# Gate and up products of two SwiGLU half steps by seven block products for eight, with the hidden tiles through DRAM to a down phase of its own

## The chip, the cores and the metric

The kernel runs on one core of a Trainium2 chip. The metric is the device time of one execution in microseconds (us). Its engines are named as in the profile: PE (TensorE, matmuls), DVE (VectorE), ACT (ScalarE), POOL (GpSimd) and SP (SyncE, which here only issues DMAs). The matmuls write into eight PSUM banks of 128 partitions by 512 float32; everything else lies in SBUF or DRAM.

## The reference

One residual block over 1024 tokens of 1024 channels, all in float32:

```python
x = x + 0.5 * swiglu(rmsnorm(x, ffn1_norm), ffn1_w_gate, ffn1_w_up, ffn1_w_down)
x = x + hybrid_mixer(rmsnorm(x, mix_norm), w_in, conv_w, conv_b, sb_out_norm, conv_out_norm, w_out)
x = x + 0.5 * swiglu(rmsnorm(x, ffn2_norm), ffn2_w_gate, ffn2_w_up, ffn2_w_down)
return rmsnorm(x, final_norm)

def swiglu(h, w_gate, w_up, w_down):
    return (silu(h @ w_gate) * (h @ w_up)) @ w_down
```

`w_gate` and `w_up` are 1024 by 2816, `w_down` is 2816 by 1024. The mixer projects to q, k, v and three convolution streams (`w_in`, 1024 by 3072), does stick-breaking attention in 8 heads of 64 and a short causal convolution over 512 channels, norms both groups, and projects back with `w_out` (1024 by 1024).

## The kernel before

**Arithmetic.** A float32 operand is split into a high part, rounded to the format float32r that PE multiplies (a CAST on ACT, line 173), and the remainder (a subtraction on DVE, line 174). A product of two operands is three matmuls, high by high, high by low, low by high (`mm3` and `both`, lines 220 to 244); each is 128 by 128 by 512 and they add up in one PSUM bank. All matmuls of the main stream are issued in `mm`, line 95.

**FFN.** Channels lie on the partitions, tokens along the row, in two halves of 512 (`hf`). The 2816 hidden channels are 22 tiles of 128, in five chunks (`CHUNKS`). For a tile `m`, `ffn` makes the gate product and then the up product, over 8 tiles of input channels and both halves (`both`): 2 x 8 x 2 x 3 = 96 matmuls into four banks. `gated` reads gate from PSUM (lines 422 to 424), `hidden` multiplies by up (432) and splits the result into an `h` tile. At the end of a chunk its down product is made for each of 8 tiles of output channels and added to the residual (463). In the second FFN the last chunk's down product has rows of tokens (`down_by_rows`), with the residual transposed on PE (`to_rows`, 891) one chunk earlier, and each row goes through the final norm and out; the very last piece is 256 columns wide.

**Norm.** `Norm.feed` splits the residual times the gain (180) without waiting for the rms. 1/rms follows through a chain of small steps (`Rms`: sums, columns, diagonals, broadcast, rows) and arrives as a row in every partition (the copy of line 312); `gated` multiplies by it. For the mixer, `rescale` scales the tiles themselves later (327).

**Weights.** `Stream` holds the order of all weight tiles. A tile of 128 by 1024 is loaded on SP's DMA queue into one of three `raw` slots and split into one of two pairs `whi`, `wlo`, one tile ahead.

**Order.** The kernel's text lays side chains between the matmuls at distances (`after`). The order on each engine's queue is made by a planner from the text's order and from when it reckons that operands and slots are ready: an instruction that isn't ready may be passed by a later one. `behind` fixes an order where it must hold. A slot of a pool is given again once all readers of its last tile are done.

**Memory.** 32 `act` slots of 512 columns (2 KB a partition) hold the split activations, 18 `h` slots of 1024 columns the hidden tiles, the residual, v, q and k, 18 `t` slots of 512 what is temporary.

## Time and profile before

| | us |
|---|---|
| median of 3 runs | 1979.15 |
| lowest, highest run | 1977.16, 1981.97 |
| span of the profiled execution | 1980.5 |
| PE busy | 1965.7 |
| weight loads (PEld) busy | 1633.7 |
| DVE busy | 931.5 |
| ACT busy | 666.3 |
| POOL busy | 46.4 |

The page gives the profiled execution no time beside its span; the span lies between the lowest and the highest run. A row of a group names the line, engine, operation, output and inputs with their shapes, how many there are, their busy time together, the mean of one in ns, and the idle time of the engine ahead of them with what ended it. A row of a window gives the stretch in us, its length, then for each engine its busy time in the stretch with the number of its instructions, the granted clock of PE, the share of the DMA engines and GB/s. A row of the timeline gives start, duration, engine, line, operation and tiles; a DMA's row among the issues gives the number, the size and the median us from issue to landing. Matmuls are pipelined, so the duration shown for one is longer than the distance between two, and the distance is what counts.

### The profile page before, as it was taken

To read this page: it belongs to the slowest core of one execution; us is meant where nothing else is said; L and a number is where in the kernel's file an instruction comes from. 1 tells how busy PE (TensorE), PEld (TensorE's weight loads), DVE (VectorE), ACT (ScalarE), POOL (GpSimd) and SP (SyncE) were. 2 spreads that over 40 slices of the span, in tenths; PEclk is the share of its full clock that TensorE was granted. 3 is DMA by queue.
4 is the path that set the end of the run, shared out by engine and by line. 5 is a ranking of instruction groups with operands and counts; after the bars stand their busy time and mean duration, and the time that the engine had idled before them with its cause. 6 is when DMAs were issued, how large, how long until landed. Compare 5 with 4: busy or idle time off the path is not lost.

```text
span 1980.5 us, 22183 instructions
## 1 busy us (share of the span) xinstructions
PE 1965.7 (99%) x8932; PEld 1633.7 (82%) x8932; DVE 931.5 (47%) x1541; ACT 666.3 (34%) x1212; POOL 46.4 (2%) x78
## 2 busy tenths in 40 slices
PE   9999999999999999999999999999999999999998
PEld 7888888888888888788888888888888888888887
DVE  6423233333333277568787898433333233333335
ACT  6311121111211155467677775321111121112223
POOL 0000000000000000100101000000000000000001
PEclk9999999999999999999999999999999999999999
DMA  5112112102112042332405222211211211201212
GB/s 160 40 39 67 47 34 63 48 27 75 32 47 65 28 160 85 83 78 56 96 27 128 91 93 65 64 35 40 64 50 33 67 43 33 74 27 52 61 43 86
DMA packets 181287, 124.15 MB, mean 63 GB/s; under 512 B 5392, under 2 KB 167488, under 8 KB 181184
## 3 DMA queue, kind: packets, MB, share of 16 engines
q1 hardware_dynamic: 177344, 113.29, 19.2%
q0 software_dynamic: 3840, 9.44, 2.4%
q8 instruction: 70, 1.15, 0.2%
q14 instruction: 33, 0.27, 0.0%
HBM read 102.00 MB, written 11.27 MB: 57 GB/s over the span
## 4 chain that ended last, share of the span: by engine, by line
PE 99%; issue 1%; DMA 0%; ACT 0%; DVE 0%; SPq 0%; POOL 0%; POOLq 0%
PE ps L95 97%; PE ps L276 0%; PE ps L891 0%; PE ps L479 0%; DMA raw<-in_ffn_w_up 0%; PE ps L304 0%; PE ps L306 0%; PE ps L307 0%; POOL sm L930 0%; ACT t L935 0%; POOLq L961 0%; DVE wlo L499 0%; DVE act L180 0%; ACT whi L496 0%; ACT t L312 0%
## 5 line engine op out<-in xcount | busy, mean ns | idle before, releaser
L95 PE MATMUL ps<-act,whi 128*128 128x512 f32 x3648 | 1037.3, 391 | 2.4 <-ACT act L179 1.6
L95 PEld LDWEIGHTS ps<-act,whi 128*128 128x128 f32 x3648 | 682.1, 188 | 139.4 <-ACT act L179 1.8
L95 PE MATMUL ps<-act,wlo 128*128 128x512 f32 x1824 | 600.0, 390 | 0.0
L173 ACT CAST whi<-raw 128x1024 fp32r<-128x1024 f32 (+2 forms) x200 | 183.1, 915 | 1107.2 <-PE ps L95 1066.0
L95 PEld LDWEIGHTS ps<-act,wlo 128*128 128x128 f32 x1824 | 342.9, 188 | 68.1 <-DVE wlo L174 0.4
L95 PE MATMUL ps<-h,whi 128*128 128x512 f32 x1344 | 362.6, 389 | 0.0
L95 PEld LDWEIGHTS ps<-h,whi 128*128 128x128 f32 x1344 | 252.1, 188 | 52.7 <-ACT h L173 0.3
L174 DVE TENSOR_TENSOR wlo<-raw,whi 128x1024 fp32r<-128x1024 f32 (+2 forms) x200 | 209.5, 1047 | 25.3 <-ACT whi L173 25.2
L463 DVE SCALAR_TENSOR_TENSOR h<-ps,h 128x512 f32<-128x512 f32 x144 | 92.8, 686 | 265.5 <-PE ps L95 265.4
L95 PE MATMUL ps<-h,wlo 128*128 128x512 f32 x672 | 209.5, 389 | 0.0
L422 DVE TENSOR_TENSOR t<-t,ps 128x512 f32<-128x512 f32 x88 | 56.5, 684 | 316.3 <-PE ps L95 316.3
L432 DVE TENSOR_TENSOR t<-t,ps 128x512 f32<-128x512 f32 x80 | 51.5, 684 | 281.4 <-PE ps L95 281.3
L95 PEld LDWEIGHTS ps<-h,wlo 128*128 128x128 f32 x672 | 126.1, 188 | 26.2
L762 ACT ACTIVATE t<-ps 128x128 f32<-128x128 f32 (+2 forms) x96 | 47.0, 489 | 43.9 <-PE ps L95 43.4
L95 PE MATMUL ps<-h,h 128*128 128x128 f32 (+2 forms) x192 | 57.8, 357 | 3.3 <-issue 3.3
L774 DVE TENSOR_TENSOR t<-t,ps 128x128 f32<-128x128 f32 (+2 forms) x96 | 52.8, 550 | 16.7 <-ACT t L770 16.3
L424 DVE TENSOR_TENSOR t<-t,t 128x512 f32<-128x512 f32 x88 | 56.7, 685 | 4.0 <-ACT t L423 4.0
L174 DVE TENSOR_TENSOR h<-t,h 128x512 fp32r<-128x512 f32 x89 | 57.4, 685 | 1.0 <-ACT h L173 1.0
L770 ACT ACTIVATE t<-t 128x128 f32<-128x128 f32 (+2 forms) x96 | 50.2, 523 | 19.1 <-DVE t L766 17.8
L807 DVE TENSOR_TENSOR t<-ps,t 128x128 fp32r<-128x128 f32 (+2 forms) x96 | 52.9, 551 | 4.7 <-ACT ps L803 4.1
L788 DVE TENSOR_TENSOR t<-t,t 128x128 fp32r<-128x128 f32 (+2 forms) x96 | 53.1, 553 | 3.7 <-ACT t L784 3.3
L173 ACT CAST h<-t 128x512 fp32r<-128x512 f32 x89 | 52.4, 618 | 4.8 <-DVE t L432 4.8
(126 smaller groups left out, 1334.2 us busy)
## 6 DMA issues: line engine op xcount, KB each, us to landing
raw<-in_ffn_w_gate SPq DMA_DIRECT2D x43, 512.0 KB, 3.9
raw<-in_ffn_w_up SPq DMA_DIRECT2D x43, 512.0 KB, 3.9
raw<-in_w_in SPq DMA_DIRECT2D x28, 512.0 KB, 4.0
raw<-in_ffn_w_down SPq DMA_DIRECT2D x32, 320.0 KB, 3.2
raw<-in_ffn_w_down SPq DMA_DIRECT2D x40, 256.0 KB, 2.8
h<-h POOLq DMA_DIRECT2D x24, 256.0 KB, 5.0
raw<-in_w_out SPq DMA_DIRECT2D x12, 512.0 KB, 3.4
h<-in_x SPq DMA_DIRECT2D x8, 512.0 KB, 7.3
```

The source lines that it names most:

```text
L95: nc.tensor.matmul(out, lhs, rhs, **kw)
L173: nc.scalar.copy(hi, x)
L174: nc.vector.tensor_tensor(out=lo, in0=x, in1=f(hi), op=ALU.subtract)
L422: nc.vector.tensor_tensor(out=s[hf], in0=rms, in1=g[hf], op=ALU.mult)
L424: nc.vector.tensor_tensor(out=s[hf], in0=s[hf], in1=rms, op=ALU.mult)
L432: nc.vector.tensor_tensor(out=s[hf], in0=s[hf], in1=u[hf], op=ALU.mult)
L463: nc.vector.scalar_tensor_tensor(out=x, in0=o[hf], scalar=0.5, in1=x, op0=ALU.mult, op1=ALU.add)
L762: behind(nc.scalar.activation(u["s"][:, cols], u["z"][:, cols], AF.Exp), table_set)
L770: nc.scalar.activation(sc, sc, AF.Ln, bias=1.0)
L774: nc.vector.tensor_tensor(out=sc, in0=sc, in1=u["z"][:, cols], op=ALU.max)
L788: nc.vector.tensor_tensor(out=u["sl"][:, cols], in0=u["s"][:, cols], in1=f(u["sh"])[:, cols], op=ALU.subtract)
L807: nc.vector.tensor_tensor(out=u["al"][:, cols], in0=u["z"][:, cols], in1=f(u["ah"])[:, cols], op=ALU.subtract)
```

## The change

**Gate and up.** In each FFN the first two hidden tiles are made as before (`STD`); in the first FFN the very first of them still runs under the transposes of the input. For the other 20 tiles, gate and up of one tile, two halves of the input channels and two halves of the tokens are seen as a 2 by 2 by 2 block product. It is made by seven products of blocks (`P1`, `P2`, `P3`, `P5`, `P6`, `P7`, `Q4`) of 4 channel tiles each, 7 x 4 x 3 = 84 matmuls, in place of eight. The right operands are sums and differences of the activations, scaled by gain and 1/rms in place, and split: 7 x 4 pairs, made once in each FFN by `right`. The left operands are sums of the four blocks of a tile's gate and up weights, made for each tile by `left` in steps, one step behind each product of the tile before. The seven products go into four banks: P2 adds to P1's, Q4 to P7's, P3 to P5's, each after the part that is there has been read (`Unit.do`). The first two Strassen tiles of a phase run product by product together (`ALL`), while the right operands are made; the others one by one (`FEW`).

**Hidden tiles.** They are stored unsplit to DRAM (`h_sp`) on POOL's DMA queue. When all 22 are made, `down` reads them back in pairs, splits them (`down_prep`) and makes all of the down product in fourteen steps (`TURNS`), each with two output tiles and up to four pairs of hidden tiles. In the first FFN the outputs are channels by tokens; in the second they are rows of tokens throughout, on the residual that `to_rows` has transposed and stored to DRAM (`r_sp`) at the end of the mixer.

**Residual.** The input's tiles are stored to DRAM at the start (`x_sp[0]`) and read back at the first four down steps (`x_back`), since `right` overwrites them.

**Slots.** The pools `act`, `h` and `t` become one pool `s` of 72 slots of 512 columns; the weights' parts are 10 slots `w` of 1024 columns; `raw` is 2 slots of 2048 columns, and a weight load can be 1 MB. q, k and their parts are tiles of one token half, and their copies between partitions are twice as many of half the size. Two of the eight v tiles lie in `s`.

```diff
-    def big(tag, bufs, dt=F32, shape=(P, S)):
-        return sb.tile(list(shape), dt, name=nm(tag), tag=tag, bufs=bufs)
-    def act_tile(dt=F32R):
-        return big("act", 32, dt, (P, HALF))
-    def h_tile(dt=F32R):
-        return big("h", 18, dt)
-    def tmp(dt=F32):
-        return big("t", 18, dt, (P, HALF))
+    def s(dt=F32):
+        return sb.tile([P, HALF], dt, name=nm("s"), tag="s", bufs=72)
+    def w4(dt=F32R):
+        return sb.tile([P, S], dt, name=nm("w"), tag="w", bufs=10)
...
+            raw = sb.tile([P, 2 * S], F32, name=nm("raw"), tag="raw", bufs=2)
+            for c0, n, view, src in spec:
+                nc.sync.dma_start(out=view(raw[:, c0 : c0 + n]), in_=src)
...
+    h_sp = [dr.tile([NF, P, S], F32, name=f"h_sp{i}") for i in range(2)]
+    NQ = NF // 2
+    TURNS = [(i % 4, max(0, i - 3), min(NQ, i + 1)) for i in range(NQ + 3)]
...
+            yield [part(j * S, w[:, m * P : (m + 1) * P]) for j, w in enumerate((wg, wu))]
+        h = h_sp[i].rearrange("f p c -> (f p) c")
+        ring, rows = (wd, h) if i else (h, wd)
+        for j, (g, q0, q1) in enumerate(TURNS):
+            if j < NQ:
+                yield [part(0, ring[2 * j * P : 2 * (j + 1) * P])]
+            yield [part(k * (q1 - q0) * 2 * P, rows[2 * q0 * P : 2 * q1 * P, (g + 4 * k) * P : (g + 4 * k + 1) * P])
+                   for k in range(2)]
...
-    def ffn(act, started, scale, last, done):
...
-        for c in range(5):
-            h = []
-            for m in range(CHUNKS[c], CHUNKS[c + 1]):
...
-                run(both(g, W(), NK, act))
...
-                s = gated(g, act)
-                run(both(u, W(), NK, act))
-                h.append(hidden(s, u, scale if c == 4 else None))
...
-            for d in range(NK):
-                w = W()
                 o = [bank(), bank()]
-                run(both(o, w, len(h), lambda k, hf: tuple(a[:, hs(hf)] for a in h[k])))
...
+    def left(raw):
+        a = {}
+        def blk(i, n=1):
+            return raw[:, i * HALF : (i + n) * HALF]
+        def halves(hi, lo, *names):
+            for i, n in enumerate(names):
+                a[n] = (hi[:, i * HALF : (i + 1) * HALF], lo[:, i * HALF : (i + 1) * HALF])
+        def two(ap):
+            return ap.rearrange("p (n c) -> p n c", c=HALF)
+        yield a
+        halves(*split(w4(), w4(), blk(0, 2)), "P2", "P1")
+        yield
+        y = w4(F32)
+        nc.vector.tensor_tensor(out=two(y), in0=two(blk(1, 2)), in1=blk(3).unsqueeze(1).to_broadcast([P, 2, HALF]),
+                                op=ALU.add)
+        nc.vector.tensor_tensor(out=blk(3), in0=y[:, :HALF], in1=blk(2), op=ALU.add)
+        nc.vector.tensor_tensor(out=blk(0), in0=blk(3), in1=blk(0), op=ALU.add)
+        yield
+        z = two(raw)[:, 0::3]
+        hi, lo = w4(), w4()
+        split(two(hi), two(lo), z)
+        halves(hi, lo, "P3", "P6")
+        yield
+        halves(*split(w4(), w4(), y), "P7", "P5")
+        yield
+        a["Q4"] = split(s(F32R), s(F32R), blk(2))
+        L.load()
+        yield
+    def right(x, y):
+        b = {}
+        yield b
+        def parts(name, tiles):
+            b[name] = [split(s(F32R), s(F32R), a) for a in tiles]
+        def comb(out, i, j, op):
+            nc.vector.tensor_tensor(out=out, in0=i, in1=j, op=op)
+            return out
+        def four(k0, hf):
+            return [y(k0 + i, hf) for i in range(4)]
+        b11 = four(4, 0)
+        parts("P1", b11)
+        yield
+        b21 = four(0, 0)
+        parts("P2", b21)
+        yield
+        b22, b12, t3 = [], [], []
+        for i in range(4):
+            b22.append(y(i, 1))
+            b12.append(y(4 + i, 1))
+            t3.append(comb(s(), b22[i], b12[i], ALU.subtract))
+        parts("P7", t3)
+        yield
+        t1 = [comb(b11[i], b11[i], b12[i], ALU.subtract) for i in range(4)]
+        parts("P5", t1)
+        yield
+        t2 = [comb(b12[i], t1[i], b22[i], ALU.add) for i in range(4)]
+        parts("P6", t2)
+        yield
+        parts("Q4", [comb(b21[i], t2[i], b21[i], ALU.subtract) for i in range(4)])
+        yield
+        parts("P3", b22)
+        yield
+    BANK = {"P1": 0, "P2": 0, "P6": 1, "P7": 2, "Q4": 2, "P5": 3, "P3": 3}
...
+    FEW, ALL = ("P1", "P6", "P2", "P7", "P5", "Q4", "P3"), ("P1", "P2", "P7", "P5", "P6", "Q4", "P3")
...
+        def do(self, name):
+            i = BANK[name]
+            first = i not in self.o
+            if first:
+                self.o[i] = bank()
+            o = self.o[i]
+            for k in range(4):
+                run(mm3(o, wk(self.a[name], k), self.b[name][k], first and k == 0,
+                        k == 3 and name in ("P2", "P6", "Q4", "P3"), skip_group_check=True))
+            self.done.add(name)
+            if name == "P1":
+                self.p1 = s()
+                nc.scalar.copy(self.p1, o)
+            if name == "P2":
+                self.s0 = s()
+                last_silu[0] = nc.scalar.activation(self.s0, o, AF.Silu)
+            if name == "P6":
+                self.u2 = self.p1
+                nc.vector.tensor_tensor(out=self.u2, in0=self.p1, in1=o, op=ALU.subtract)
+            if name in ("P6", "P7") and {"P6", "P7"} <= self.done:
+                self.u3 = s()
+                nc.vector.tensor_tensor(out=self.u3, in0=self.u2, in1=self.o[2], op=ALU.add)
+            if name in ("P6", "P7", "P5") and {"P6", "P7", "P5"} <= self.done:
+                nc.vector.tensor_tensor(out=self.u3, in0=self.u3, in1=self.o[3], op=ALU.add)
+            if name == "Q4":
+                u = s()
+                nc.vector.tensor_tensor(out=u, in0=self.u2, in1=o, op=ALU.add)
+                self.store(0, u, self.s0)
+            if name == "P3":
+                nc.vector.tensor_tensor(out=self.u2, in0=self.u2, in1=o, op=ALU.add)
+                last_silu[0] = nc.scalar.activation(self.u2, self.u2, AF.Silu)
+                self.store(1, self.u3, self.u2)
+        def store(self, hf, u, g):
+            nc.vector.scalar_tensor_tensor(out=u, in0=u, scalar=-1.0, in1=g, op0=ALU.mult, op1=ALU.mult)
+            nc.gpsimd.dma_start(out=self.out[:, hs(hf)], in_=u)
...
+        rights = right(act.x, normed_in_place)
+        b = next(rights)
+        preps = [left(L.take()[0]) for _ in range(2)]
+        units = [Unit(next(p), b, out[nstd + j]) for j, p in enumerate(preps)]
+        for p in preps:
+            next(p)
+        for name in ALL:
+            next(rights)
+            for p in preps:
+                next(p, None)
+            for u in units:
+                u.do(name)
+        act.x.clear()
+        x_tiles.clear()
+        prep = left(L.take()[0])
+        a = next(prep)
+        run(prep)
+        for m in range(nstd + 2, NF):
+            unit = Unit(a, b, out[m])
+            if m + 1 < NF:
+                prep = left(L.take()[0])
+                a = next(prep)
             else:
...
+                prep = down_prep(0)
+            for name in FEW:
+                unit.do(name)
+                next(prep, None)
+            run(prep)
...
+    def down_prep(j):
+        if j < NQ:
+            raw, _ = L.take()
+            ring[j] = {}
+            for i in range(4):
+                ring[j][divmod(i, 2)] = split(s(F32R), s(F32R), raw[:, hs(i)])
+                yield
+            L.load()
+        raw, n = L.take()
+        rows_of[j] = []
+        for i in range(2):
+            c = slice(i * n // 2, (i + 1) * n // 2)
+            rows_of[j].append(split(w4()[:, : n // 2], w4()[:, : n // 2], raw[:, c]))
+            yield
+        L.load()
+    def down(flush, start=None):
+        for j, (g, q0, q1) in enumerate(TURNS):
+            prep = down_prep(j + 1) if j + 1 < len(TURNS) else iter(())
+            if start:
+                start(j)
+            last = j >= NQ - 1
+            for i in range(2):
                 o = [bank(), bank()]
+                n = (q1 - q0) * 2
+                for k in range(n):
+                    hi, lo = (a[:, k * P : (k + 1) * P] for a in rows_of[j][i])
+                    for hf in range(2):
+                        run(mm3(o[hf], (hi, lo), ring[q0 + k // 2][k % 2, hf], k == 0, k == n - 1))
+                    if k % 2:
+                        next(prep, None)
+                flush(j, g, i, o)
+            run(prep)
...
     def rows_in(hf, c):
-        xr[hf, c] = h_tile(F32).rearrange("p (j c) -> p j c", j=4)
...
+        for j in range(2):
+            xr[hf, c, j] = s().rearrange("p (j c) -> p j c", j=2)
...
     def turn(k, hf):
...
+        nc.gpsimd.dma_start(out=x_sp[0][k][:, hs(hf)], in_=x)
...
+    def x_back(j):
+        if j < 4:
+            for i in range(2):
+                for hf in range(2):
+                    d = j + 4 * i
+                    nc.sync.dma_start(out=xT(d, hf), in_=x_sp[0][d][:, hs(hf)])
...
+            r = s()
+            nc.scalar.copy(r, tp)
+            nc.gpsimd.dma_start(out=r_sp[4 * hf + j][:, hs(i)], in_=r)
...
+    def to_output(j, g, i, o):
+        tt = g + 4 * i
+        for hf in range(2):
+            r = rows[tt, hf]
+            nc.vector.scalar_tensor_tensor(out=r, in0=o[hf], scalar=0.5, in1=r, op0=ALU.mult, op1=ALU.add)
+        if j < NQ - 1:
+            return
```

More of the change, by code (lines that the diff above doesn't have):

```diff
@@ L467, in hybrid_block @@
     x_in = t["x"][0]
+    x_sp = [dr.tile([NK, P, S], F32, name=f"x_sp{i}") for i in range(2)]
     act0 = Norm("ffn1_norm")
@@ L483, in turn @@
         (nc.scalar.copy if k % 2 else nc.vector.tensor_copy)(x, tp)
+        nc.gpsimd.dma_start(out=x_sp[0][k][:, hs(hf)], in_=x)
         return last
-    w0 = [(next(W.specs)[0], big("raw", 3), big("whi", 2, F32R), big("wlo", 2, F32R)) for _ in range(2)]
+    w0 = [(t[f"ffn1_w_{n}"][0][:, :P], w4(F32), w4(), w4()) for n in ("gate", "up")]
     def w0_in(part):
@@ L653, in x_load @@
     def x_load(hf):
-        for q in range(4):
-            xT(2 * q, hf)
-            nc.sync.dma_start(out=x_tiles[q, hf], in_=x_sp[q, hf])
+        for d in range(NK):
+            nc.sync.dma_start(out=xT(d, hf), in_=x_sp[1][d][:, hs(hf)])
     def w_out_part(k0, halves):
```

379 lines of the change are left out of this document (192 added, 187 removed).

## The prediction

> **What bounds the kernel now.** I read the page first: busy times, slices, chain of waits.
>
> ```profile
> span 1980.5 us, 22183 instructions
> ...
> PE 1965.7 (99%) x8932; PEld 1633.7 (82%) x8932; DVE 931.5 (47%) x1541; ACT 666.3 (34%) x1212; POOL 46.4 (2%) x78
> ...
> PE 99%; issue 1%; DMA 0%; ACT 0%; DVE 0%; SPq 0%; POOL 0%; POOLq 0%
> ```
>
> TensorE (PE) is busy 99% of the span, and the chain that ends last is 99% PE. VectorE (DVE) and ScalarE (ACT) are under half busy. So a matmul less is time less, as long as the others keep PE fed. Next I took the stages in windows, and two read-outs of the second FFN in order of time.
>
> ```profile
> core 0: us, PE busy (x) PEld busy (x) DVE busy (x) ACT busy (x) POOL busy (x), PEclk, DMA share, GB/s
> 100.00:700.00 600.00, 600.00 (x2649) 496.82 (x2648) 196.66 (x283) 103.49 (x146) 1.47 (x6) 1.00 0.16 47
> 750.00:1130.00 380.00, 376.74 (x1826) 319.06 (x1825) 287.03 (x554) 255.57 (x542) 25.83 (x49) 1.00 0.32 81
> 44.60:62.40 17.80, 17.80 (x84) 14.80 (x83) 9.16 (x17) 8.90 (x18) 1.02 (x1) 1.00 0.05 15
> 1257.80:1291.40 33.60, 33.60 (x150) 27.81 (x149) 10.97 (x15) 7.89 (x11) 0.00 (x0) 1.00 0.16 47
> ```
> ```profile
> 1280.55 1.28 DVE L422 TENSOR_TENSOR t<-t,ps 128x512 f32<-128x512 f32 x2 [7.26 <-PE ps L95]
> ...
> 1291.43 1.29 DVE L432 TENSOR_TENSOR t<-t,ps 128x512 f32<-128x512 f32 x2 [7.25 <-PE ps L95]
> ```
>
> In an FFN, PE never stops (600.00 of 600 us, granted clock 1.00), DVE works a third of it, DMA a sixth. From the one read-out (of gate) to the next (of up) there are 48 matmuls and 10.88 us: **0.2267 us a matmul**, and 2.72 us for a block product of 12.
>
> **What goes: 108.8 us.** A tile of 128 hidden channels takes 2 weights x 8 input tiles x 2 token halves x 3 = 96 matmuls now, and 7 products x 4 x 3 = 84 then. It is used for 20 of 22 tiles in each FFN, so 40 x 12 = 480 matmuls go: 480 x 0.2267 = 108.8 us. The down phase keeps its 1056 matmuls per FFN (the fourteen steps of TURNS add to 44 pairs x 2 x 2 x 2 x 3), the attention its own.
>
> [...]
>
> **What is added, by engine.** Prices of like instructions:
>
> ```profile
> L174 DVE TENSOR_TENSOR wlo<-raw,whi 128x1024 fp32r<-128x1024 f32 x128 | 156.0, 1219 | 25.3 <-ACT whi L173 25.2
> L173 ACT CAST whi<-raw 128x1024 fp32r<-128x1024 f32 x128 | 134.8, 1053 | 694.2 <-PE ps L95 671.3 <-issue 22.5 <-ACT t L267 0.3
> L174 DVE TENSOR_TENSOR h<-t,h 128x512 fp32r<-128x512 f32 x89 | 57.4, 685 | 1.0 <-ACT h L173 1.0
> L173 ACT CAST h<-t 128x512 fp32r<-128x512 f32 x89 | 52.4, 618 | 4.8 <-DVE t L432 4.8
> L422 DVE TENSOR_TENSOR t<-t,ps 128x512 f32<-128x512 f32 x88 | 56.5, 684 | 316.3 <-PE ps L95 316.3
> L423 ACT ACTIVATE t<-t 128x512 f32<-128x512 f32 x88 | 52.6, 628 | 2.1 <-DVE t L422 2.1
> L312 ACT COPY t<-ps 128x512 f32<-128x512 f32 x10 | 5.8, 581 | 3.6 <-PE ps L304 2.0 <-PE ps L307 1.5
> L327 DVE SCALAR_TENSOR_TENSOR t<-h,gains,t 128x512 f32<-128x512 f32 x16 | 11.3, 747 | 3.6 <-ACT t L312 3.6
> ```
>
> *A tile in the steady state.* left() on DVE: three remainders and one sum of 1024 columns, 4 x 1.22, and two sums and a remainder of 512, 3 x 0.685: 6.9 us. Unit's read-out: 7 x 0.685 = 4.8 us. That is 11.7 us of DVE, and 3 x 1.05 + 0.62 + 0.58 + 2 x 0.63 = 5.6 us of ACT, under 84 x 0.2267 = 19.0 us of PE. The sum of busy time is covered; the places where PE could wait are Q4, which goes on in the bank of P7 once DVE has read it, and P3, which goes on in the bank of P5. One product, 2.72 us, lies between in each case. Behind P5 on DVE stand a remainder (1.22; of the ten w slots eleven would be wanted here, so it waits until P5 frees one) and the sum (0.69): 1.9 us, so 0.8 us is left. I take 0 for the 36 such tiles; the other end is one such 1.22 us more at one place in each, less the 0.8 us: 36 x 0.4 = 15 us.
>
> *The start of each Strassen phase.* Here seven sets of right operands are made once, for two tiles whose products alternate. On DVE: P1 and P2 four scalings (0.747) and four remainders each, 5.7 us each; P7 eight scalings, four differences, four remainders, 11.5; P5, P6, Q4 5.5 each; P3 2.7; two left() 13.9; two read-outs 9.6. Sum 65.6 us, against 2 x 19.04 = 38.1 us of PE. **In this stage DVE is the bound.** The step that decides is P7. Before its first product DVE needs, in order, 2.4 (first splits) + 5.7 + 5.2 (sums) + 5.7 + 2.4 + 11.5 + 1.2 = 34.2 us, and 1.4 us for the hidden tile of the last standard product; PE has only the four products P1 and P2, 10.9 us. What helps is what DVE can do ahead. The queue isn't kept in the order of the text: a read-out of a later tile went ahead of an older product.
>
> ```profile
> 54.59 1.88 DVE L422 TENSOR_TENSOR t<-t,ps 128x512 f32<-128x512 f32 x3
> ...
> 57.59 0.68 DVE L432 TENSOR_TENSOR t<-t,ps 128x512 f32<-128x512 f32 x1
> ...
> 62.48 1.28 DVE L432 TENSOR_TENSOR t<-t,ps 128x512 f32<-128x512 f32 x2 [1.87 <-PE ps L95]
> ```
> ```profile
> 44.00 0.59 ACT L312 COPY t<-ps 128x512 f32<-128x512 f32 x1
> ...
> 1257.17 0.59 ACT L312 COPY t<-ps 128x512 f32<-128x512 f32 x1 [1.23 <-PE ps L307]
> ```
>
> The scalings need the row of 1/rms, and it is there at 44.6 us in the first FFN (its first half) and at 1257.8 in the second; the second tile's products end at 62.4 and 1291.4. In the windows above DVE is free 17.8 - 9.2 = 8.6 us there, and 33.6 - 11.0 = 22.6 us here; what the change drops from the windows (one weight split 1.2, two remainders 1.4) adds 2.6 each. So some 11 us are done ahead in the first FFN; in the second 25 by that count, and I take 23, since the s slots (72, of which activations and residual hold 48 until the last standard product) bound it. P7 then starts 35.6 - 11 = 24.6 us behind the last standard product in the first FFN, 13.7 us late, and 12.6 in the second, 1.7 late. Behind it P6 and Q4 wait for their four sums and first remainder, about 3 us more each time. I take **16 + 5 = 21 us**. Bounds: if nothing is done ahead, 16 + 11 = 27 and 5 + 23 = 28, 55 us; at best the second is free and the first keeps the 13.7 us that no idle time covers.
>
> A PE that stands for 13 us is a thing that this trace doesn't show; its granted clock is 1.00 in every FFN window. [...]
>
> *Into and through the down phase.* Tiles that stayed in SBUF now go to DRAM (44 stores of 256 KB per FFN on POOL's queue) and come back on SP's.
>
> ```profile
> raw<-in_ffn_w_gate SPq DMA_DIRECT2D x43, 512.0 KB, 3.9
> ...
> raw<-in_ffn_w_down SPq DMA_DIRECT2D x40, 256.0 KB, 2.8
> h<-h POOLq DMA_DIRECT2D x24, 256.0 KB, 5.0
> ...
> h<-x_sp SPq DMA_DIRECT2D x8, 512.0 KB, 5.5
> ```
>
> By the third row a store lands in about 5 us; tiles come back two a step from the first on, so even the last pair has eight steps, over 150 us, between store and load. From 256 to 512 KB costs 1.1 us, so 1 MB takes some 6 us by these rows, up to 11 by twice the slowest. A full step has 96 matmuls, 21.8 us, with two such loads and 4 x 0.69 + 2 x 1.22 + 4 x 0.69 = 8.0 us of DVE: covered. The first three steps have 24, 48 and 72 matmuls, 5.4, 10.9 and 16.3 us. In the first, DVE must still store the last tile (2.7), split six blocks of 512 (4.1): 6.9 us in 5.4. In the next, a load can only start when its one of two raw slots is split. I take **3 us for each FFN**, 6; bounds 0 and 2 x 10, when a load of 11 us stands open in the first two steps.
>
> *Start, mixer, end.*
>
> ```profile
> 0.81 0.43 SPq L473 DMA_DIRECT2D h<-in_x  x1
> ```
> ```profile
> 2.23 4.84 DMA raw<-in_ffn_w_up
> ```
> ```profile
> 1973.80 0.41 DVE L918 TENSOR_TENSOR t<-h,ps 128x256 f32<-128x256 f32 x1
> ```
>
> One more issue (0.43) stands ahead of the first weights, whose landing the first products wait for, and 16 stores of x run beside the loads: 1 us, bounds 0 and 4. The last read-out is 512 columns for 256 and in two halves: 0.69 for 0.41, its square and scaling alike, and the row of tokens before it (some 3.2 us of DVE in the last half step of 2.7): 2 us, bounds 1 and 4. The transposes to rows are moved, not added. In the mixer the slots are pooled and q goes in twice as many, half as large copies on POOL's queue; by the window from 750 PE is idle there 3.3 of 380 us. 0 us, bounds -3 and +10.
>
> **Sum.** 1980.5 - 108.8 + 21 + 6 + 1 + 2 = 1901.7. The profile gives the execution no time beside its span; that is 1.35 us over the median of the runs (1979.15). So 1900.
>
> **Rivals.**
> *The start is covered better* (0.17): the second FFN's 5 and the down phases' 6 vanish. For it: 25 us of free DVE there, DMA at a sixth. 1889 us.
> *Nothing is made ahead* (0.2): slots or the planner's order keep the right operands behind the last standard product: 21 becomes 55, 1934 us. For it: 48 of 72 slots held; against it, the order of the rows at 54.59 and 57.59.
> *Slower: DVE reads the banks late in each steady tile* (0.06). If preparation lies in one lump ahead of the read of P7 (sums 2.6, two remainders 2.4, the read 0.7: 5.7 us for a cover of 2.7) PE waits 3 us, 36 x 3 = 108 us: 2008. It decides from 2.2 us a tile, (1979 - 1900)/36. Against it: DVE has 7 us free in 19, and reads wait ahead of preparation that isn't due.
>
> **How the numbers follow.** The forecast itself has 0.53; its own range is 1889 to 1920. 0.04 is left for mixer or start going badly in other ways. The bounds that can meet on the high side (55 for 21, 15 in the tiles) give 1949, of which the range leaves out the last 3; its low end takes the better start, the mixer's 3 us and 6 of the first FFN's 16: 1880. Range 1880 to 1946. A measurement tells about 0.2% from no change. Faster 0.92, within it 0.02, slower 0.06, nearly all from the slower rival.
>
> **What would show it.** PE's count falls by 480 to about 8450, at 0.2267 us in the steady tiles, each 19.0 us between stores. PE idles behind the second standard tile, released by DVE, about 16 us in the first FFN and 5 in the second, most of it ahead of P7. Small gaps stand in the first two down steps, released by DVE or DMA. It is wrong if the wait at the start is under 10 or over 40 us, if steady tiles take over 19.5 us, or if the mixer, the start or the end move by over 5 us.

## The result, and the profile after

The changed kernel takes 1919.74 us (median of 4 runs, 1919.51 to 1920.08) against 1978.98 us before (4 runs, 1977.16 to 1981.97). The ratio is 0.970, with a 95% interval of 0.9688 to 0.9715: 3.0% faster. The forecast was 1900. All working below goes by the profiled executions: 1980.5 us before, 1918.0 after. In every run with both figures the span is 1.7 to 2.0 us below the execution's time (1918.0 for 1919.72), so the execution profiled before was about the slowest of its four, some 3 us over their median: the spans differ by 62.5 us, the medians by 59.2.

The page of the changed kernel, first its busy times and slices, then the shares of the chain that ended last:

```profile
PE 1872.8 (98%) x8440; PEld 1549.3 (81%) x8440; DVE 1182.9 (62%) x1829; ACT 770.4 (40%) x1366; POOL 133.0 (7%) x238
...
PE   6989999999999999999999999999999999999997
...
PEclk8989999999999999999999999999999999999999
...
PE 91%; DVE 5%; issue 1%; ACT 1%; DMA 1%; SPq 0%; POOL 0%; POOLq 0%; DVEq 0%; ACTq 0%
```

PE has 492 matmul records less (480 were predicted; the other 12 are the last piece of the down product, 24 matmuls of 256 columns before for 12 of 512). PE's row has two weak places at the left, in the first and third slice, and the granted clock falls in the same two. The chain, 99% PE before, now has 9% of other work in it. So most of the loss sits in the first 150 us, and the steady stages should look like the prediction. They do:

```profile
core 0: us, PE busy (x) PEld busy (x) DVE busy (x) ACT busy (x) POOL busy (x), PEclk, DMA share, GB/s
200.00:300.00 100.00, 100.00 (x443) 82.81 (x442) 58.14 (x72) 28.07 (x38) 5.40 (x10) 1.00 0.27 81
480.00:700.00 220.00, 220.00 (x973) 182.15 (x972) 87.60 (x123) 51.20 (x76) 4.32 (x8) 1.00 0.38 121
1320.00:1660.00 340.00, 340.00 (x1501) 281.30 (x1500) 204.83 (x261) 97.45 (x134) 20.50 (x38) 1.00 0.28 86
```

These windows are Strassen tiles of the first FFN, its down phase, and Strassen tiles of the second. PE is busy in every microsecond of all three, at clock 1.00.

To see where the 62.5 us went, four marks divide the span: the read-out behind the second hidden tile (62.48 us before, in the prediction), the read-out behind the first hidden tile of the second FFN, PE's end, and the span's end. The rows are from the timelines, first of the kernel before, then of the changed one:

```profile
1269.67 1.28 DVE L432 TENSOR_TENSOR t<-t,ps 128x512 f32<-128x512 f32 x2 [6.75 <-PE ps L95]
...
1973.34 0.28 PE L95 MATMUL ps<-whi,h 128*128 128x256 f32 x1
```
```profile
86.79 1.27 DVE L579 TENSOR_TENSOR s<-s,ps 128x512 f32<-128x512 f32 x2
...
154.15 0.69 DVE L562 TENSOR_TENSOR s<-s,ps 128x512 f32<-128x512 f32 x1
173.19 0.69 DVE L562 TENSOR_TENSOR s<-s,ps 128x512 f32<-128x512 f32 x1
...
1257.35 1.27 DVE L579 TENSOR_TENSOR s<-s,ps 128x512 f32<-128x512 f32 x2
...
1278.69 1.28 DVE L579 TENSOR_TENSOR s<-s,ps 128x512 f32<-128x512 f32 x2 [2.44 <-PE ps L91]
...
1894.77 11.49 PE L91 MATMUL ps<-s,w 128*128 128x512 f32 x50
```

| stretch | before | after | difference | the prediction's terms |
|---|---|---|---|---|
| start to the second tile's end | 62.5 | 86.8 | **+24.3** | +1 |
| to the first tile of the second FFN | 1207.2 | 1170.6 | -36.6 | -54.4 + 16 + 3 = -35.4 |
| to PE's end | 703.9 | 648.9 | -55.0 | -54.4 + 5 + 3 = -46.4 |
| PE's end to the span's end | 6.9 | 11.7 | **+4.9** | +2 |

A steady Strassen tile takes 173.19 - 154.15 = 19.04 us, 84 x 0.2267. The 64 transposes to rows (some 7 us) lie in the second stretch now and in the third before, which the terms above don't hold. Each mark is that of one execution. The first row of the table is the one that was missed.

**What happens at the start.** ScalarE's queue and PE in the changed kernel's timeline, and behind them a row of ScalarE from the kernel before:

```profile
8.57 0.68 ACT L175 ACTIVATE s<-ps,gains 128x512 fp32r<-128x512 f32 x1
22.59 1.04 ACT L169 CAST w<-raw 128x1024 fp32r<-128x1024 f32 x1 [13.34 <-DMA raw<-in_ffn_w_gate]
23.54 0.68 ACT L175 ACTIVATE s<-ps,gains 128x512 fp32r<-128x512 f32 x1
...
24.28 0.79 PE L91 MATMUL ps<-s,w 128*128 128x512 f32 x1 [11.19 <-ACT s L175]
```
```profile
34.07 1.06 ACT L173 CAST whi<-raw 128x1024 fp32r<-128x1024 f32 x1 [0.37 <-PE ps L95]
```

The first row is a feed (`scaled_split`) of an input tile for the first hidden tile's products. The next instruction in ScalarE's queue is the split of the **second** tile's gate weights. It waits 13.34 us for a load that was issued behind all rows of the input; the second feed, whose rows were there, stands behind it until 23.54, and PE waits 11.19 us for that feed. In the kernel before, the first such whole split started at 34.07 us, since its slot had to come free first. Now there are ten w slots, of which the first tile holds six, and the planner put the split ahead. That the free slots are what let it do so is read from the pools and the queue; no run takes the slots away.

Then the clock falls. Windows of the changed kernel (columns as above), in the startup and in the first Strassen start:

```profile
28.00:30.00 2.00, 2.00 (x8) 1.75 (x7) 1.02 (x3) 1.00 (x2) 0.54 (x1) 0.50 1.16 323
95.00:100.00 5.00, 5.00 (x16) 3.91 (x15) 5.00 (x9) 0.00 (x0) 0.00 (x0) 0.66 0.01 3
100.00:104.00 4.00, 1.35 (x7) 0.80 (x6) 4.00 (x6) 3.73 (x6) 0.00 (x0) 1.00 0.00 0
...
108.00:112.00 4.00, 4.00 (x11) 3.14 (x11) 4.00 (x8) 2.41 (x5) 0.00 (x0) 0.50 0.00 0
```

From about 17 to 30 us the clock is 0.50, 6 us of it with PE at work again. It falls again in a wait of 2.83 us for the sums of the norm (58.46 us), and twice in the Strassen start: from 95 to 99 us, behind waits of 1.25 and 0.50 us, and from 105 to 112, after PE was a third busy from 100 to 104. The kernel before has 1.00 over its first 800 us.

**The two Strassen starts.** PE's rows with their waits, first and second FFN of the changed kernel:

```profile
93.01 0.74 PE L91 MATMUL ps<-s,w 128*128 128x512 f32 x2 [1.25 <-ACT s L169]
...
103.81 0.73 PE L91 MATMUL ps<-s,w 128*128 128x512 f32 x2 [2.65 <-ACT s L169]
106.63 21.53 PE L91 MATMUL ps<-s,w 128*128 128x512 f32 x82 [2.09 <-DVE s L170]
...
1285.56 6.02 PE L91 MATMUL ps<-s,w 128*128 128x512 f32 x24 [1.24 <-ACT s L169]
1293.34 0.73 PE L91 MATMUL ps<-s,w 128*128 128x512 f32 x2 [1.76 <-ACT s L169]
1295.41 18.93 PE L91 MATMUL ps<-s,w 128*128 128x512 f32 x82 [1.33 <-DVE s L170]
```

The same two places stall in both, P2 and P7. What each start costs in all is measured by the run with eight products, next.

### The profile page after: what moved, and what is told of

Read it like the earlier page. It is cut to its first block, busy times and chain, and to the rows that moved or that the text cites. A ratio compares the mean times of both kernels' runs of the same rounds, so it can differ in the third digit from the quotient of the medians.

```text
span 1918.0 us, 22275 instructions
## 1 busy us (share of the span) xinstructions
PE 1872.8 (98%) x8440; PEld 1549.3 (81%) x8440; DVE 1182.9 (62%) x1829; ACT 770.4 (40%) x1366; POOL 133.0 (7%) x238
## 4 chain that ended last, share of the span: by engine, by line
PE 91%; DVE 5%; issue 1%; ACT 1%; DMA 1%; SPq 0%; POOL 0%; POOLq 0%; DVEq 0%; ACTq 0%
PE ps L91 89%; DVE s L170 1%; DMA raw<-in_ffn_w_gate 1%; DVE w L170 1%; DVE s L269 0%; DVE s L496 0%; PE ps L277 0%; DVE s L595 0%; DVE s L176 0%; PE ps L853 0%; DMA s<-in_x 0%; SPq L677 0%; ACT w L169 0%; PE ps L683 0%; DVE s L875 0%
## 5 line engine op out<-in xcount | busy, mean ns | idle before, releaser
L91 PE MATMUL ps<-s,w 128*128 128x512 f32 x6880 | 1623.1, 391 | 25.9 <-ACT s L175 11.7
L91 PEld LDWEIGHTS ps<-s,w 128*128 128x128 f32 x6880 | 1286.0, 189 | 294.2 <-ACT s L175 12.6
L169 ACT CAST w<-raw 128x1024 fp32r<-128x1024 f32 (+3 forms) x182 | 181.1, 996 | 493.8 <-PE ps L91 339.6
L170 DVE TENSOR_TENSOR w<-raw,w 128x1024 fp32r<-128x1024 f32 (+3 forms) x182 | 209.2, 1151 | 138.4 <-ACT w L169 80.1
L91 PE MATMUL ps<-s,s 128*128 128x512 f32 (+3 forms) x704 | 179.0, 375 | 2.0 <-DVE s L170 1.0
L91 PEld LDWEIGHTS ps<-s,s 128*128 128x128 f32 x704 | 132.0, 188 | 29.3 <-DVE s L170 1.8
L170 DVE TENSOR_TENSOR s<-raw,s 128x512 fp32r<-128x512 f32 x128 | 85.0, 684 | 56.0 <-ACT s L169 56.0
L169 ACT CAST s<-raw 128x512 fp32r<-128x512 f32 x128 | 74.6, 617 | 85.0 <-DMA raw<-in_ffn_w_down 46.7
L766 DVE SCALAR_TENSOR_TENSOR s<-ps,s 128x512 f32<-128x512 f32 x56 | 38.0, 688 | 97.7 <-PE ps L91 97.3
L1134 DVE SCALAR_TENSOR_TENSOR s<-ps,s 128x512 f32<-128x512 f32 x56 | 37.9, 687 | 93.5 <-PE ps L91 93.4
L170 DVE TENSOR_TENSOR w<-w,w 128x1024 fp32r<-128x1024 f32 x40 | 49.0, 1224 | 41.2 <-PE ps L91 39.0
L170 DVE TENSOR_TENSOR s<-s,s 128x512 fp32r<-128x512 f32 x88 | 58.4, 682 | 5.6 <-ACT s L169 5.5
```

The source lines that it names most:

```text
L91: nc.tensor.matmul(out, lhs, rhs, **kw)
L169: nc.scalar.copy(hi, x)
L170: nc.vector.tensor_tensor(out=lo, in0=x, in1=f(hi), op=ALU.subtract)
L766: nc.vector.scalar_tensor_tensor(out=x, in0=o[hf], scalar=0.5, in1=x, op0=ALU.mult, op1=ALU.add)
L1134: nc.vector.scalar_tensor_tensor(out=r, in0=o[hf], scalar=0.5, in1=r, op0=ALU.mult, op1=ALU.add)
```

## The experiments

All ratios are to the kernel before, on the same chip, with their 95% intervals; the changed kernel itself has 0.9701 (0.9688 to 0.9715).

| run | time, us | ratio |
|---|---|---|
| e3_std22, all tiles with eight products | 2006.41 | 1.0147 (1.0132 to 1.0162) |
| e1_hold, second tile's splits held | 1906.98 | 0.9644 (0.9629 to 0.9658) |
| e5_hold_d20, and squares earlier | 1906.24 | 0.9630 (0.9616 to 0.9645) |
| e9_hold_late30, and copies later | 1898.00 | 0.9597 (0.9582 to 0.9611) |
| e2_swap, P7/P5 split ahead of P3/P6 | 1918.72 | 0.9699 (0.9683 to 0.9716) |
| e4_std3, three standard tiles | 1921.21 | 0.9715 (0.9700 to 0.9729) |
| e6_ahead, operands one product earlier | 1912.36 | 0.9661 (0.9647 to 0.9676) |
| e6_ahead_swap, both | 1914.34 | 0.9672 (0.9656 to 0.9688) |
| e7_all, held, earlier, swapped | 1900.49 | 0.9600 (0.9586 to 0.9615) |
| e8_hold_ahead_std32 | 1887.07 | 0.9544 (0.9529 to 0.9558) |
| e10_best | 1881.84 | 0.9512 (0.9496 to 0.9527) |
| e11_short_stores | 1882.46 | 0.9506 (0.9486 to 0.9526) |

### The seven products undone

```diff
-    STD = (2, 2)
+    STD = (NF, NF)
...
+        if nstd == NF:
+            act.x.clear()
+            x_tiles.clear()
+            run(down_prep(0))
+            return
```

> All 22 tiles of each FFN by eight block products (the two standard ones made 22), with the tiles through DRAM, the separate down phase, the startup and the tail as in the changed kernel: the seven products alone are undone. Theory A (the changed kernel is 108.8 us of matmuls saved, less 14.5 us of waits in the two Strassen starts, and the rest of what was lost, some 32 us of startup and tail, has nothing to do with the seven products): 1919.7 + 108.8 - 14.5 = 2014 us, within 4, that is 35 us slower than the kernel before. Rival B (the startup loss comes from the Strassen phase's larger loads, 1 MB for 512 KB): the second tile's products end near 65 us, and the time is 1990 to 1997.

Measured: 2006.41, 29 us slower than the kernel before. Theory A by its sign, but 7.6 us off its number, which it gave within 4; rival B fell, since the second tile still ends at 84.11:

```profile
84.11 1.29 DVE L579 TENSOR_TENSOR s<-s,ps 128x512 f32<-128x512 f32 x2 [3.26 <-PE ps L91]
...
1295.89 1.28 DVE L579 TENSOR_TENSOR s<-s,ps 128x512 f32<-128x512 f32 x2 [6.79 <-PE ps L91]
1317.65 1.28 DVE L579 TENSOR_TENSOR s<-s,ps 128x512 f32<-128x512 f32 x2 [7.26 <-PE ps L91]
...
1859.64 132.76 PE L91 MATMUL ps<-s,w 128*128 128x512 f32 x585
```

A tile is 1317.65 - 1295.89 = 21.76 us, 96 x 0.2267, and nothing waits at the change to the down phase: from 1317.65, 20 tiles and 1056 matmuls of the down phase make 435.2 + 239.4 = 674.6 us, and PE ends at 1992.40, 674.75 later. In the first FFN PE is busy 279.60 of the 280 us from 520, which hold its change to the down phase. So **going through DRAM and the separate down phase cost nothing**, and this kernel prices the Strassen stage. From the second tile to the first of the second FFN it takes 1211.8 us, the changed kernel 1170.6: 41.2 saved of 54.4, so the first start costs **13.2 us**. From the second tile of the second FFN to PE's end it takes 674.75 against 627.57: 47.2 saved, so the second start costs **7.2 us**. The expectation had 14.5 for both, counted to a read-out that in the paired tiles stands two products before their end; 20.4 is the right sum, and that is most of its miss.

### The startup

First, the splits of the second tile held behind the last feed (`inst` is the copy on ScalarE in `split`):

```diff
+        if hold[0] is not None:
+            behind(inst, hold[0])
...
+    hold[0] = last_scaled[0]
     W.prepare()
+    hold[0] = None
```

> The splits of the second tile's weights are kept behind the last feed of the input (a wait in the text's order alone; no work is added or left out). Theory A (the order of ScalarE's queue): the 24 us that the end of the second tile's products came late, at 86.8 us for 62.5, go back to 0 to 4 us, the granted clock stays 1.00 over the first 80 us, the row of 1/rms of the first half is there at about 45 us again, and the first Strassen pair finds its scalings partly made, as before the tile ends: 1893 to 1900 us. Rival B (the DMA queue: rows of the input in 16 pieces for 8, and 16 stores of x beside them): the feeds wait for rows instead, the start stays over 15 us late, and the time stays within 8 us of 1919.7.

Measured: 1906.98, 12.8 us faster than the changed kernel; the second tile ends at 72.82 for 86.79. The order of ScalarE's queue is a cause, the rival falls, but theory A promised 62 to 66. What is left shows in this run's windows and in ScalarE's timeline:

```profile
10.00:30.00 20.00, 20.00 (x107) 16.37 (x105) 11.77 (x19) 11.08 (x19) 5.57 (x10) 1.00 0.99 336
30.00:60.00 30.00, 26.80 (x110) 21.15 (x109) 21.13 (x36) 19.77 (x39) 6.24 (x8) 0.89 0.41 125
```
```profile
31.80 0.59 ACT L692 COPY s<-ps 128x512 f32<-128x512 f32 x1 [1.52 <-DVE s L180]
...
43.76 1.83 PE L281 MATMUL ps<-ones_r,s 128*128 128x1 f32 x8 [2.83 <-DVE s L273]
...
72.82 1.28 DVE L583 TENSOR_TENSOR s<-s,ps 128x512 f32<-128x512 f32 x2
```

PE now works from 10 to 30 us, but waits 2.83 us for the sums of the norm, with half clock behind it (0.50 from 44 to 50 us). The squares (L272) come late, and ScalarE idles 0.35 to 1.52 us at each copy of x (L692) until VectorE has made the remainder of the same turn (L180; a turn transposes and feeds one input tile). Two edits tell these apart. The squares alone:

```diff
-        act0.feed(k, hf, tp, x, 45 if hf else 50)
+        act0.feed(k, hf, tp, x, 20 if hf else 20)
```

> As the run with the held weight splits (1907.0 us), and the squares of the input, for the sums behind 1/rms, stand 20 matmuls behind their feed in the text for 45 to 50; no work is added or left out. With the splits held, the second tile's products still ended 10.3 us later than in the kernel before: the first sum waited 2.83 us for squares that ScalarE took up late, and the granted clock then fell to half. Theory A (those late squares are the rest): no wait at the sums, clock 1.00 over the first 70 us, the second tile's products end at 62 to 67 us, 1897 to 1901 us. Rival B (the first tile's own products, 3.7 us later, and what follows from the pieces of the row loads): a late end of 70 us or more stays, 1903 to 1907 us.

Measured: 1906.24, the second tile at 72.86. The wait only moved from the sums to the feeds; theory A of that run fell. Then the copies of odd `k`, left over to the next turn, where `copies()` makes them and their stores, with the squares 30 matmuls behind their feeds:

```diff
-        (nc.scalar.copy if k % 2 else nc.vector.tensor_copy)(x, tp)
-        nc.gpsimd.dma_start(out=x_sp[0][k][:, hs(hf)], in_=x)
+        copies()
+        if k % 2 and (k, hf) != (NK - 1, 1):
+            late.append((k, hf, x, tp))
+        else:
+            copy(k, hf, x, tp)
```

> Held weight splits; the copy of x from PSUM that ScalarE makes for every second turn stands behind the feed of the next turn in the text, and the squares stand 30 matmuls behind their feeds for 45 to 50: ScalarE's queue is then nearly that of the kernel before. With the splits held alone, ScalarE waited 0.8 to 1.5 us at each such copy for VectorE's remainder of the same turn, both engines in step, and squares alone moved up gave nothing. Theory A (this lockstep makes the rest of the startup's loss): the second tile's products end at 63 to 68 us for 72.8, no wait over 1 us on PE from 10 to 60 us, 1898 to 1902 us. Rival B (the row loads in 16 pieces and the 16 stores make it): 70 us or more, 1904 to 1908 us.

Measured: 1898.00, and the second tile ends at 64.19, 1.7 us behind the kernel before, with clock 1.00 from 10 to 60 us:

```profile
30.00:60.00 30.00, 29.54 (x138) 23.80 (x137) 26.50 (x45) 23.00 (x46) 7.68 (x9) 1.00 0.41 132
...
64.19 1.28 DVE L583 TENSOR_TENSOR s<-s,ps 128x512 f32<-128x512 f32 x2
```

Theory A held. With the row loads still in 16 pieces and the 16 stores of x still there, of the 24.3 us 22.6 are gone: **they were the order of ScalarE's queue**, 14.0 the split that stood ahead, 8.6 the two engines in step, each with the half clock that followed. These are marks of single executions: in the six kernels whose startup has the text of the changed one, itself among them, the second tile ends at 84.11 to 88.58 us. The squares moved together with the copies in the last run; moved alone, to 20 matmuls, they had given nothing.

### The starts of the Strassen phases

I had three suspects: VectorE's time (the prediction's), the ten w slots, and again ScalarE's queue. The slots, in `left` for the two paired tiles:

```diff
-        hi, lo = w4(), w4()
-        split(two(hi), two(lo), z)
-        halves(hi, lo, "P3", "P6")
-        yield
-        halves(*split(w4(), w4(), y), "P7", "P5")
-        yield
+
+        def z_part():
+            hi, lo = w4(), w4()
+            split(two(hi), two(lo), z)
+            halves(hi, lo, "P3", "P6")
+
+        def y_part():
+            halves(*split(w4(), w4(), y), "P7", "P5")
+
+        for fn in (y_part, z_part) if y_first else (z_part, y_part):
+            fn()
+            yield
...
-        preps = [left(L.take()[0]) for _ in range(2)]
+        preps = [left(L.take()[0], True) for _ in range(2)]
```

> For the two tiles of each phase that run together, the parts of P7 and P5 are split before those of P3 and P6; nothing else changes. Theory A (the ten w slots): P1/P2 of two tiles hold four slots, the two sums two, and the parts of P3/P6 take the last four, so the split for P7 waits until P2 has given slots back; with the order swapped it takes the last four itself. The waits at P7 (1.24 and 1.76 us on ScalarE's split in the second FFN, 2.65 in the first) go, and come back smaller at P6, which is two products later: 3 to 7 us less, 1913 to 1917 us. Rival B (VectorE's time alone decides): P7's other operands come no earlier, under 1 us: 1919 to 1921.

Measured: 1918.72. The interval of its ratio covers that of the changed kernel: the order in which w slots are taken is not it. VectorE's time:

```diff
-    STD = (2, 2)
+    STD = (3, 3)
```

> Three standard tiles for two in each FFN: 24 more matmuls, 5.4 us, and 21.8 us more of standard products ahead of each Strassen start, of which VectorE needs about 6.5. Theory A (VectorE's time bounds the start in the first FFN; slots s leave room for the right operands of P1 and P2 at least, 11.4 us): the start's 10 us in the first FFN fall to 2 to 5, the second FFN's 4.5, held by slots w, stays: 1918 to 1922 us. Rival B (slots bound both starts): both stay, 1925 us. Rival C (VectorE's time bounds both): both go, 1911 to 1914.

Measured: 1921.21, 1.5 more with 5.4 us more of matmuls, so 3.9 us of waiting went. The first FFN's start now shows the second's pattern:

```profile
115.50 5.99 PE L91 MATMUL ps<-s,w 128*128 128x512 f32 x24 [1.19 <-ACT s L169]
123.26 0.73 PE L91 MATMUL ps<-s,w 128*128 128x512 f32 x2 [1.76 <-ACT s L169]
125.33 20.52 PE L91 MATMUL ps<-s,w 128*128 128x512 f32 x82 [1.33 <-DVE s L170]
```

So VectorE's time made the difference between the two starts, theory A, and something that spare VectorE time doesn't touch made the rest. The queues of ScalarE and VectorE, in the second FFN of the changed kernel, say what:

```profile
1284.40 0.59 ACT L548 COPY s<-ps 128x512 f32<-128x512 f32 x1 [2.13 <-PE ps L91]
1284.89 2.18 ACT L169 CAST s<-s 128x512 fp32r<-128x512 f32 x4
...
1285.54 2.50 DVE L170 TENSOR_TENSOR s<-s,s 128x512 fp32r<-128x512 f32 x4 [4.42 <-ACT s L169]
```

L548 reads the banks of P1 and waits for PE. The four splits for P2, ready long before, stand behind it, so PE ends P1 with nothing to go on with. VectorE idles 4.42 us for the same splits, and that time is missing when it prepares P7: in the 5 us from 1291, where PE waits, it is busy throughout. One step earlier in the text, `step()` being the three lines taken out of the loop:

```diff
+        step()
         for name in ALL:
-            next(rights)
-            for p in preps:
-                next(p, None)
+            step()
             for u in units:
                 u.do(name)
```

> In the two tiles that run together, the text prepares the operands one product earlier (those of P1 and P2 ahead of P1); nothing else changes. Theory A (the order of ScalarE's queue: the splits for P2 stand behind the copies of P1's banks, which wait for PE): PE's gap ahead of P2 goes (1.24 us in the second FFN, 1.25 in the first, each with some 0.5 us of restart), the waits for w slots and for VectorE stay: 1915 to 1918 us. Rival B (slots bound the start alone): the gap moves to the next product, 1919 to 1921 us.

Measured: 1912.36, 7.4 us less, better than theory A. This window of the second FFN's start has no stall left (the changed kernel has PE at 45.67 of 50 us in it), and the first FFN's wait has moved to P7:

```profile
1260.00:1310.00 50.00, 50.00 (x220) 40.78 (x219) 42.76 (x66) 24.06 (x41) 1.08 (x2) 1.00 0.19 53
...
105.09 21.45 PE L91 MATMUL ps<-s,w 128*128 128x512 f32 x82 [4.89 <-DVE s L170]
```

From the second tile of the second FFN (1276.94) to PE's end (1897.75) this run takes 620.8 us for the changed kernel's 627.57. So nearly all of the second start's 7.2 us, 6.8, was the order; the waits at P7 went with it, though no slot was added. The edit moves the work of both engines; that it is ScalarE's queue that counts is read from the rows above, where VectorE waits for it. In the first FFN the edit gained nothing (1171.0 us between the marks for 1170.6). Both edits together, and then with the startup's first two:

> The earlier text and the swapped splits (P7 and P5 ahead of P3 and P6) together. Swapped alone gave 1 us. Theory A (queue order and w slots each hold the second FFN's start, VectorE's time the first's): the second FFN's start, 7.2 us over its matmuls, falls to 0 to 2.5, the first's falls by 1 to 3: 1910 to 1914 us. Rival B (VectorE's time bounds both): 1916 to 1920 us.

Measured: 1914.34, just above theory A's 1910 to 1914, and 2.0 more than without the swap, with intervals that overlap: the swap is worth nothing here either.

> Held weight splits, squares 20 matmuls behind, earlier text, swapped splits, and in the last step of the last down phase the two token halves of the last row one after the other for interleaved, so that half of the read-out lies under products. If the causes add: 1919.7 less 20 (startup), 7 (starts of both phases) and 1 (tail): 1889 to 1895 us. If the two starts only hand the wait on to VectorE's time: 1896 to 1900 us.

Measured: 1900.49. The two groups of edits add up to less than hoped, close to the second case expected: in the first FFN PE still waits 5.21 and 2.07 us for VectorE. That leaves VectorE's time there, which three standard tiles for two in that FFN alone should cover, with the held splits and the earlier text:

```diff
-    STD = (2, 2)
+    STD = (3, 2)
```

> Held weight splits and the earlier text (without the swap), and three standard tiles in the first FFN, two in the second. The earlier text took the second FFN's start to nothing, 7.4 us of the time; in the first FFN VectorE is busy throughout and the wait only moved. Theory A (VectorE's time bounds the first FFN's start): one standard tile more gives it 21.8 us, of which the tile takes some 6.5; the start falls from 11 to 13 us to 0 to 3, and the lost saving of 12 matmuls costs 2.7: 1889 to 1893 us. Rival B (the slots or ScalarE's queue hold that start too): 1899 to 1904 us.

Measured: 1887.07, and in both starts PE is busy throughout:

```profile
95.00:150.00 55.00, 55.00 (x243) 44.87 (x242) 49.99 (x72) 26.06 (x41) 2.71 (x5) 1.00 0.36 105
...
1230.00:1330.00 100.00, 100.00 (x441) 82.20 (x440) 82.61 (x118) 38.82 (x60) 5.64 (x11) 1.00 0.27 79
```

Theory A, 1.9 us better than its range. In the changed kernel VectorE is busy in every microsecond from 86 to 116; the windows at 95, 100 and 108 us above show 5.00 of 5, 4.00 of 4 and 4.00 of 4. So **VectorE's time bounds the first FFN's start, ScalarE's order the second's**.

### All together, and the end

The held splits, the late copies, the earlier text, three standard tiles in the first FFN, and for the last row of the last step one half after the other:

```diff
...
-                for k in range(n):
+                end = i and j == len(TURNS) - 1
+                for k, hf in ([(k, hf) for hf in range(2) for k in range(n)] if end else
+                              [(k, hf) for k in range(n) for hf in range(2)]):
...
```

> All of it: held splits, late copies with squares 30 behind, earlier text, three standard tiles in the first FFN, and the halves of the last row one after the other. If the causes add: 1880 to 1886 us, under both kernels. If the late copies give nothing: 1888 to 1892 us.

Measured: 1881.84, 4.9% under the kernel before and 2.0% under the changed one. From the kernel before's 1980.5 one expects 1980.5 - 108.8 + 2.7 (one tile more by eight products) = 1874.4; the profiled execution took 1881.0. Of the 6.6 us between them, 4.8 are at the end: 11.7 us from PE's end to the span's end, as in the changed kernel, for 6.9 before. The last edit above left that end as it was. The startup has 2.6 more (the second tile ends at 65.12).

```diff
+            n = HALF if j < len(TURNS) - 1 else 64
-            nc.sync.dma_start(out=out[tt * P : (tt + 1) * P, hs(hf)], in_=r)
+            nc.sync.dma_start(out=out[tt * P : (tt + 1) * P, hf * HALF : hf * HALF + n], in_=r[:, :n])
```

> The kernel with all edits (1881.8 us), and the four stores of the last down step write 64 of each 512 columns: the rest of these two rows of the output is left out, all arithmetic stays. It measures what lies between PE's end and the span's end, 11.7 us in it and in the changed kernel, 6.9 in the kernel before. Theory A (the 1 MB of the last four stores, 0.5 MB before, sets the end): 8.5 to 9.5 us from PE's end, 1878.5 to 1880 us. Rival B (the chain of read-out, square, power and scaling, and the fixed time of a store after it): 11 us or more, 1881 to 1882.5.

Measured: 1882.46, 11.7 us again (PE ends at 1869.0 of 1880.7). The size of the last stores is not it. The last stores are issued like this, first in the kernel before, then in the changed one:

```profile
1976.58 0.87 SPq L936 DMA_DIRECT2D out_y<-t  x2
```
```profile
1910.79 0.81 SPq L1158 DMA_DIRECT2D out_y<-s  x2
```

PE ends at 1906.26, the last store is issued by 1911.6, and the span ends at 1918.0. The first part is the chain of read-out, square, power and scaling, over two halves of 512 columns. Behind the last issue 6.4 us pass, where the kernel before has 3.0, so 3.4 of the tail's 4.9 us lie there. In windows of half a microsecond data move until about 1913.1; in the last 4.9 us they show no data and no busy engine (1.9 us such in the kernel before). What fills them no run settles.

## Why the prediction was right, and where it was wrong

The direction was right, and so was the main mechanism: PE bounds the kernel, and the matmuls taken out come off its time. The sum was 16 us too low, 1901.7 for 1918.0 in the profiled executions. By its own signs one thing went wrong: the start moved by over 5 us. Point by point:

- **108.8 us of matmuls go.** Right: 19.04 us a steady tile against 21.76 with eight products.
- **Steady tiles, 0 us.** Right; the slower rival (VectorE reads late in each tile) is refuted by 100.00 of 100 and 340.00 of 340 us.
- **Into and through the down phase, 6 us.** It was nothing, as the run with eight products shows: 674.75 us where the matmuls alone make 674.6.
- **The start in the first FFN, 16 us, bound by VectorE.** Right in cause, 13.2 in size. VectorE is busy throughout from 86 to 116 us, and one more standard tile ahead of it, with ScalarE's order mended, takes the start to nothing. Of the 13.2 some 4.6 are half clock (an estimate: half of the 9.1 us that PE worked at 0.50 in it), which the prediction's sum has no term for, so the waits alone are nearer 9 than 16. Part of the reason is the price, which was a little high: I took mean durations of 0.685 us, but instructions that follow each other start closer. Four differences of 512 columns show 2.49 us together, so three distances of 0.60 and one duration.

```profile
1291.12 2.49 DVE L496 TENSOR_TENSOR s<-s,s 128x512 f32<-128x512 f32 x4
```

- **The start in the second FFN, 5 us, bound by VectorE and by s slots.** It was 7.2 us, near in size, which was luck, but **wrong in cause**: preparing the operands one product earlier in the text took 6.8 of it, with the same slots and the same VectorE work. The step that failed is "What helps is what DVE can do ahead": I counted VectorE's free time and not what stands ahead of a split in ScalarE's queue. "Nothing is made ahead" (1934) didn't come either; P1's operands were.
- **Startup, 1 us, bounds 0 and 4.** This step failed: 24.3 us. I priced one more issue on SP's queue and 16 stores, and looked at the startup only for what the change adds there. What it changes is which slots are free: with ten w slots the second tile's weights no longer wait for a slot, and the planner sent their split ahead of the feeds. Holding it and putting the copies later took 22.6 of the 24.3 away, with the added issue and stores in place, so my term for these, 1, was about right (1.7 us are left); the missing term is the order.
- **Half clock.** The sum has no term for it, and the kernel before, at 1.00 in every window of the prediction, gave no price. In the changed kernel it came: 0.50 from 16.74 us on, within the 11.19 us wait, and for 6 us of work after. The two Strassen starts show what it costs: behind the wait at P7, 82 matmuls take 21.53 us in the first, with the clock at 0.50 up to 112.32 us, and 18.93 in the second, at 1.00, so 2.60 of 5.69 us were lost. By the estimate used above, half, it cost some 5.8 us in the startup and 4.6 in the first Strassen start.
- **Tail, 2 us, bounds 1 and 4.** Mis-sized: 4.9. The chain of the last read-out was counted, not what lies behind the last issue, 3.4 of the 4.9, whose cause stays open.
- **Mixer, 0.** Right. With eight products, the stretches from the second tile's end to PE's end sum to 2.8 us less than in the kernel before (1211.8 + 696.5 against 1207.2 + 703.9), within the bounds of -3 and +10. Most of this need not be the change: the execution profiled before has in its mixer one wait of PE of 3.27 us, at 813.14, that ends with nothing the profile shows and has half clock behind it (0.71 from 814 to 815 us, 0.54 from 816 to 818). The changed kernel's has none (1.00 from 113 to 1911 us).

In the sum: 1901.7 + 23.3 (startup) - 0.6 (starts, 20.4 for 21) - 6 (down) + 2.9 (tail) - 2.8 (mixer and the rest) = 1918.5, against 1918.0. The missed startup, 23.3, is more than the whole difference of 16.3; that the other misses come to -6.5 hid part of it, and that is luck.

## What to carry to other kernels

A larger or pooled buffer removes waits for slots, and with them an order that those waits had been keeping: after such a change, read what stands ahead of each instruction on the critical path in its engine's queue, and tie early work that waits for a late load behind what PE needs first. An engine that is half idle can still be the bound through its order: at a start, list its queue with what each entry waits for, and put the splits for the next product ahead of the copies that wait for this one. And if time goes missing after a change, look in the slices for where PE's row and its clock dip together, before doubting the steady state.

## What the runs showed of the hardware that I had not expected

In the run with held splits and earlier squares the granted clock fell without one long idle stretch. PE was 62% busy from 28 to 32 us and its longest wait there was 1.00 us, at 32.51; the clock was at 0.50 from 32.47 to 39.30:

```profile
28.00:32.00 4.00, 2.47 (x9) 1.00 (x7) 2.70 (x5) 2.48 (x6) 1.29 (x3) 1.00 0.33 128
```

In the second FFN's start of the changed kernel PE was busy 38% of 5 us, and the clock stayed at 1.00:

```profile
1291.00:1296.00 5.00, 1.90 (x8) 0.96 (x7) 5.00 (x9) 4.76 (x9) 0.00 (x0) 1.00 0.00 0
```

What may differ is where a gap lies. Read from windows of 0.5 us, the clock of the changed kernel changes at 16.74, 30.40, 57.70, 64.53, 95.25, 98.66, 105.49, 112.32 and 1911.14 us, all whole multiples of 3.4133 us apart. Read from windows of 2 us, that of e1_hold changes at 43.68, 50.52, 81.24, 84.64, 91.48 and 98.32, and that of e5_hold_d20 at 32.47, 39.30, 49.52 and 52.96: such a grid each, but shifted. The first fall is at about 17.2 us in e2_swap and 15.4 in e3_std22 (0.72 and 0.54 over 15 to 20 us), whose startups have the same text. The second FFN's start of e9_hold_late30 has the waits of the changed kernel, but there the clock fell (0.97 over 1230 to 1330 us), and the 82 matmuls behind them take 21.56 us for 18.93:

```profile
1270.72 0.73 PE L91 MATMUL ps<-s,w 128*128 128x512 f32 x2 [1.77 <-ACT s L171]
1272.79 21.56 PE L91 MATMUL ps<-s,w 128*128 128x512 f32 x82 [1.33 <-DVE s L174]
```

So the same gaps counted in one run and not in another; that their place on the grid decided it, no run isolates. Whether the busy share of PE decides it these runs don't settle either: between two points of the grid PE was 55% busy where the clock then fell (29.06 to 32.47 us in e5_hold_d20) and 49% where it stayed (1289.92 to 1293.33 in the changed kernel). A gap in PE thus cost its own length in these runs and, at times, a half clock of 3.41, 6.83 or 13.66 us (changed kernel), of which about half was lost while PE worked (2.60 of 5.69 us in the first Strassen start; an estimate from that: 1.7 us of each 3.41).

At the very start the row of the clock doesn't tell the speed: six matmuls of 512 columns take 2.93 us at 9.30 and 1.64 us at 38.58 in the changed kernel, both at a granted clock of 1.00.
